# Down projections of a hybrid encoder layer: pair 17 in seven products in both runs, pair 19 in the second

## The chip, the core and the metric

The kernel runs on one core of a Trainium2 chip. Its engines work beside each other and meet at semaphores: TensorE (PE; its weight loads are shown as PEld), VectorE (DVE), ScalarE (ACT), GpSimd (POOL) and SyncE (SP). SP issues most of the transfers (DMA) from and to the chip's memory (DRAM). POOL issues those that add to what lies in on-chip memory already. The metric is the device time of one execution in microseconds (us).

## What is computed

One encoder layer for 256 tokens of width 2048 in float32. Two feed-forward layers (FFN 1 and FFN 2, hidden width 5632) stand around a mixer of a gated recurrence and windowed attention:

```python
def swiglu(x, w_gate_up, w_down):
    gate, up = jnp.split(x @ w_gate_up, 2, axis=-1)
    return (jax.nn.silu(gate) * up) @ w_down
...
ff = swiglu(rms_norm(x, pre_norm_ffn1[layer]), w_ffn1_gate_up[layer], w_ffn1_down[layer])
x = x + 0.5 * rms_norm(ff, post_norm_ffn1[layer])
...
mixed = jnp.concatenate([y_h.astype(x.dtype), y_a.astype(x.dtype)], axis=-1) @ w_mix_out[layer]
x = x + rms_norm(mixed, post_norm_mix[layer])
ff = swiglu(rms_norm(x, pre_norm_ffn2[layer]), w_ffn2_gate_up[layer], w_ffn2_down[layer])
x = x + 0.5 * rms_norm(ff, post_norm_ffn2[layer])
```

The change touches the down projections, `(silu(gate) * up) @ w_down`, of both FFNs: 256 x 5632 times 5632 x 2048.

## The kernel before

**Numbers in two parts.** Every float32 operand is split into a high part (a cast on ACT, tile `h`) and what is left (a subtraction on DVE, tile `l`); `split_act` (L176) does both, `split_half` (L169) for 1024 columns. A product of two operands is three matmuls, high by high, high by low and low by high (`three`, L452). All of them show line L458.

**Runs, pairs and steps.** A down projection goes over its output in two runs, columns 0 to 1023 and 1024 to 2047. The hidden width is cut into 22 pairs of 128-row blocks (`NU`), numbered 0 to 21. The lists `orders` (L1276) say in which order each run takes the pairs. A step is one pair in one run, so there are 44 steps; step i is at place i in the first run, and at place i - 22 in the second. One step's weights are one 1 MB load into a `raw` tile, and there are five such tiles. The hidden activations of a pair are a tile `ht`, already split. Pairs 0 to 7 are put away to DRAM and fetched again (`fetch_at`, L1382) into four tiles that take turns; the others stay in on-chip memory.

**Plain or in seven.** A plain pair multiplies its 2 x 2 blocks of tokens and rows with its blocks of columns one by one: 8 products, 24 matmuls (`play`, `plain`). A pair in seven uses a Strassen-like scheme with 7 products, 21 matmuls (`products` of `Blocks`, L505): sums of weight blocks and sums of token blocks are multiplied, some of the products go to four extra banks `p`, and `fold` (L533) adds these to the results once, after the last pair in seven. `as_seven` (L1290) says which pairs are done so: before the change the even ones 0 to 18 (`MIXED`) in both runs and 17 in the second.

**What a pair in seven needs.** The token sums (four sums of 128 x 128): for pairs 0 to 14 they are made while the hidden activations are, and kept in the place of the residual `X`; for 16, 17 and 18 `sums_again` (L1102) makes them on DVE, after the step that `again_at` (L1384) names. At each use they are split once more (`left_sums`, L657, tile `sp`). The weight sums: for pairs in `added` (L1281) `prepare` (L1310) first splits the first weight block (tiles `ha` and `la`, L1306; three of each) four steps ahead, and then POOL issues a transfer (L1314) that reads 0.5 MB of the weights once more and adds it to the upper half of `raw`. For the others DVE does that addition (L1337). In `splits` (L1320) the lower half of `raw` is then split (`l` of the lower half), the token sums too, two more additions follow on DVE (L1342, L1343), and then the upper half and the lower half again are split. So a pair in seven has three `h` and three `l` tiles of 1024 columns, a plain pair two of each; there are five tiles of either kind in all.

**Order of loads.** A `raw` tile is loaded anew as soon as its step's last split is through (`load_down`, L1293, on SP). Which step's weights come next is set by a list sorted by place, in which the pairs of `added` count as 3.5 places earlier:

```python
in_order = sorted(
    (i - 3.5 if u in added[r] else i, i) for i, (r, u) in enumerate(steps)
)
```

**Order of work.** The loop over the steps is written out by hand (`manual_schedule`): each engine does its instructions in the order in which the program states them. At step i it states: the first part of the splits of step i + 1, `prepare(i + 4)`, the fetches due at i, the rest of those splits for a plain pair, the products of step i, the rest of the splits for a pair in seven, and then the token sums due at i. After step 21 the first run's results are squared and scaled out of their banks (`second_run`, L721). Steps 42 and 43 (pairs 20 and 21) are held for the end, where the residual is added and the next stage begins (`finish`, L743). There the residual is loaded again (`new_x`) into the place where the token sums of pairs 0 to 14 lay.

Of the kernel before, what the change touches and what calls it, by code (L numbers as in the profile page):

```python
# [37 lines left out]
def hymba_layer_kernel(  # L38
# [900 lines left out]
    MIXED = range(0, 20, 2)  # L939
# [142 lines left out]
    def ffn(gated, w_dn, post_gain, again, gain=None, lead=None, aside=None):  # L1082

        with ExitStack() as st:
# [6 lines left out]
            hts, sums, away = [], {}, {}  # L1091
# [98 lines left out]
            def some(steps, n):  # L1190
                for _ in range(n):
                    next(steps)
# [21 lines left out]
            def boundary(g, ahead):  # L1214

                a, b = room_for("z"), room_for("s")
                c, (p1, p5, p6, p7) = gated.c, gated.p
                add = nc.vector.tensor_tensor
                rest_of = gated.take(g, last)

                def bank(m, n):
                    for k in range(2):
                        rest_of[4 * k + 2 * m + n]()

                nc.scalar.copy(a, p1)
                add(c[0][0], c[0][0], a, ALU.add)
                add(b, p6, a, ALU.add)
                add(a, p7, b, ALU.add)
                add(c[1][0], c[1][0], a, ALU.add)  # L1229
                bank(0, 0)  # L1230
                bank(1, 0)
                add(b, p5, b, ALU.subtract)
                add(c[0][1], c[0][1], b, ALU.add)
                bank(0, 1)
                add(b, p5, a, ALU.subtract)
                add(c[1][1], c[1][1], b, ALU.add)  # L1236
                bank(1, 1)
                some(ahead, 2)

            def first_pairs(g, waiting):  # L1240

                gated.group(g)
                some(waiting, 1)
                gated.prepare(g, MIXED_IN[1])
                some(waiting, 1)
                ahead = gated.splits(g, 1)
                some(ahead, 2)
                gated.prepare(g, MIXED_IN[2])
                for one in gated.take(g, 0):
                    one()  # L1250
                some(waiting, 1)
                ahead = gated.splits(g, 2)
                some(ahead, 2)
                some(waiting, 1)
                some(ahead, 1)
                for one in gated.take(g, 1):
                    one()

            def pair_ahead(g, u):

                ahead = gated.splits(g, u + 1)
                next(ahead)
                if u + 1 == MIXED_IN[1]:
                    gated.prepare(g, MIXED_IN[3])
                next(ahead)
                for one in gated.take(g, u):
                    one()
                for _ in ahead:
                    pass
                if g == 1 and u == 5:  # L1270
                    sums_in(MIXED_IN[3])
                if u == 5 and 1 < g <= AWAY // 2 + 1:
                    put_away(2 * g - 4)
                    put_away(2 * g - 3)

            orders = [  # L1276
                [9, 11, 8, 13, 10, 15, 12, 1, 0, 3, 14, 5, 16, 17, 2, 7, 4, 19, 6, 18, 20, 21],

                [2, 7, 4, 9, 6, 8, 11, 10, 13, 12, 17, 15, 0, 5, 14, 3, 16, 1, 18, 19, 20, 21],
            ]  # L1280
            added = {0: (12, 0, 14, 16, 2, 4, 6, 18), 1: (*MIXED, 17)}  # L1281
            steps = [(r, u) for r in range(2) for u in orders[r]]
            in_order = sorted(
                (i - 3.5 if u in added[r] else i, i) for i, (r, u) in enumerate(steps)
# [3 lines left out]
            rows = None  # L1288

            def as_seven(r, u):  # L1290
                return u in MIXED or r == 1 and u in added[1]

            def load_down(raw):  # L1293
                if coming and (coming[0] < NU + 19 or any(raw is one for one in gated.lasting)):
# [25 lines left out]
            def splits(i):  # L1320
                if i >= 2 * NU - Pairs.HELD:
                    return
                r, u = steps[i]
                raw = raws[i]
                parts = got[i] = []
                b11, b12, b21, b22 = blocks(raw)
                if not as_seven(r, u):
                    parts.append(split_half(raw, 0))
                    yield
                    parts.append(split_half(raw, 1))  # L1330
                    load_down(raw)
                    yield
                    return
                four = raw.rearrange("p (i c) -> p i c", i=4)
                if i not in firsts:
                    first_block(i)
                    nc.vector.tensor_tensor(  # L1337
                        four[:, 0:2], four[:, 0::3], four[:, 1:2].to_broadcast([P, 2, 512]), ALU.add
                    )
                parts.append(split_half(raw, 1))  # L1340
                rows.left_sums_ahead(u)
                nc.vector.tensor_tensor(b22, b11, b22, ALU.add)  # L1342
                nc.vector.tensor_tensor(b21, b22, b21, ALU.add)  # L1343
                yield
                parts.append(split_half(raw, 0))
                yield
                parts.append(split_half(raw, 1))
                load_down(raw)
                yield
# [13 lines left out]
            with tc.manual_schedule():  # L1363
                gated.prepare(1, MIXED_IN[0])
                some(gated.splits(1, 0), 2)
                for g in range(1, NG):
                    first_pairs(g, waiting)
                    for u in range(2, last - 1):
                        pair_ahead(g, u)
                    some(gated.splits(g, last), 2)  # L1370
                    if g < NG - 1:
                        gated.prepare(g + 1, MIXED_IN[0])
                    for one in gated.take(g, last - 1):
                        one()
                    boundary(g, gated.splits(g + 1, 0) if g < NG - 1 else splits(0))
                    waiting = units(gated.c, rest)
                    some(waiting, 2)
                room_cm.__exit__(None, None, None)
                close_far()
                back_cm = tc.tile_pool(name=nm("hb"), bufs=AWAY // 2, reuse_waits="tile")  # L1380
                back = back_cm.__enter__()
                fetch_at = {2: (1,), 3: (0,), 5: (3,), 6: (5,), 9: (2,), 10: (7,), 11: (4,), 13: (6,)}  # L1382
                fetch_at.update({25: (0,), 26: (5,), 28: (3,), 29: (1,)})
                again_at = {8: 16, 14: 18, 24: 17}  # L1384
                for u in MIXED[8:]:
                    sums[u] = None
                rows = Pairs(w_dn, orders, hts, sums, work, post_gain, near=MIXED[:2])
                rows.firsts = 3
                some(waiting, 2)
                ahead = splits(1)  # L1390
                some(ahead, 2)
                products(0)
                for _ in range(2):
                    load_down(back.tile([P, 2048], F32, tag="raw", name=nm("raw"), bufs=2))
                some(waiting, 1)
                ahead = splits(2)
                some(ahead, 2)
                some(waiting, 1)
                some(ahead, 1)
                products(1)  # L1400
                for i in range(2, 2 * NU - Pairs.HELD):
                    if i == NU + 18:
                        back_cm.__exit__(None, None, None)
                        early_cm.__exit__(None, None, None)
                        post = rows.post = st.enter_context(post_pool())
                    ahead = splits(i + 1)
                    next(ahead, None)
                    prepare(i + 4)
                    for u in fetch_at.get(i, ()):
                        fetch(u)  # L1410
                    next(ahead, None)
                    if i == NU + 18:
                        rows.hold(1, raws[2 * NU - 2])
                    products(i)
                    for _ in ahead:
                        pass
                    if i in again_at:
                        sums[again_at[i]] = sums_again(again_at[i])
                    if i == 8:
                        rows.half_gain(far["pool"])  # L1420
                    if i == NU - 1:
                        sums[17] = None
                        rows.second_run()
                        rows.fold_after(NU - Pairs.HELD - 1)
                fold = rows.fold()
                some(fold, 2)
                rows.hold(1, raws[2 * NU - 1])
                for _ in fold:
                    pass
# [951 lines left out]
```

## Time and profile before

| what | us |
|---|---|
| median of three runs | 1815.16 (1814.6 to 1816.67) |
| the profiled execution | 1816.97 |
| its span, first to last instruction | 1815.2 |
| FFN 1, first run, steps 0 to 21 | 476.5 to 590.1 |
| FFN 1, second run, steps 22 to 41 | 590.1 to 691.8 |
| FFN 2, first run, steps 0 to 21 | 1580.8 to 1694.5 |
| FFN 2, second run, steps 22 to 41 | 1694.5 to 1796.2 |

All times of the trace count from the first instruction of the profiled execution. In rows of time the columns are start, duration, engine, line, operation, output <- inputs, shapes, and in brackets how long the engine was idle before and what ended that. In rows of a stage the columns are the stage, its length, the busy time of PE, PEld, DVE, ACT and POOL with the number of instructions, the granted TensorE clock, the busy share of the 16 DMA engines, and GB/s; that share goes a little over 1 where transfers are dense. Matmul durations are those of a pipeline: each is shown with 389 ns, and the next begins 227 ns after it. The start of an `l` row and the next row's start show how long DVE was really taken.

### The profile page before, as it was taken

To read this page: it belongs to the slowest core of one execution; us is meant where nothing else is said; L and a number is where in the kernel's file an instruction comes from. 1 tells how busy PE (TensorE), PEld (TensorE's weight loads), DVE (VectorE), ACT (ScalarE), POOL (GpSimd) and SP (SyncE) were. 2 spreads that over 40 slices of the span, in tenths; PEclk is the share of its full clock that TensorE was granted. 3 is DMA by queue.
4 is the path that set the end of the run, shared out by engine and by line. 5 is a ranking of instruction groups with operands and counts; after the bars stand their busy time and mean duration, and the time that the engine had idled before them with its cause. 6 is when DMAs were issued, how large, how long until landed. Compare 5 with 4: busy or idle time off the path is not lost.

```text
span 1815.2 us, 23684 instructions
## 1 busy us (share of the span) xinstructions
PE 1802.6 (99%) x8412; PEld 1496.8 (82%) x8412; DVE 1645.7 (91%) x2149; ACT 1128.2 (62%) x1496; POOL 177.9 (10%) x168
## 2 busy tenths in 40 slices
PE   9999999999999999999999999999999999999998
PEld 7888888888888888888888888888888888888886
DVE  7999999999989988988888888899999999998987
ACT  7565666666565757556676666566666666566663
POOL 1011111111011100110000100111111111011110
PEclk9999999999999999999999999999999999999999
DMA  8889999999699996965655767889999998699994
GB/s 302 240 237 282 276 283 255 254 257 260 212 343 279 280 323 208 296 174 163 174 162 166 245 206 276 244 244 270 284 268 272 255 249 251 192 337 311 263 315 164
DMA packets 217335, 457.06 MB, mean 252 GB/s; under 512 B 13064, under 2 KB 49760, under 8 KB 215936
## 3 DMA queue, kind: packets, MB, share of 16 engines
q1 hardware_dynamic: 181600, 389.07, 61.6%
q0 software_dynamic: 35440, 66.21, 21.4%
q8 instruction: 66, 1.08, 0.2%
q14 instruction: 53, 0.43, 0.1%
q10 hardware_dynamic: 176, 0.27, 0.0%
HBM read 440.80 MB, written 14.70 MB: 251 GB/s over the span
## 4 chain that ended last, share of the span: by engine, by line
PE 88%; DMA 4%; DVE 4%; ACT 2%; issue 1%; SPq 0%; POOL 0%; DVEq 0%; ACTq 0%; POOLq 0%
PE pa L458 40%; PE pb L458 35%; PE pa L326 5%; PE pa L331 3%; DMA raw<-in_w_ffn_gate_up_dram 2%; DVE l L178 2%; DMA raw<-in_w_mix_in_dram 2%; ACT h L177 1%; PE pb L1728 1%; PE pa L1172 1%; PE pb L1172 1%; DMA vr<-in_w_mix_in_dram 1%; PE pa L381 0%; ACT xt L228 0%; PE pa L380 0%
## 5 line engine op out<-in xcount | busy, mean ns | idle before, releaser
L177 ACT CAST h<-raw 128x1024 fp32r<-128x1024 f32 (+1 forms) x846 | 833.0, 1011 | 455.7 <-PE pb L458 152.4
L178 DVE TENSOR_TENSOR l<-raw,h 128x1024 fp32r<-128x1024 f32 (+1 forms) x846 | 963.0, 1170 | 97.6 <-ACT h L177 79.1
L458 PE MATMUL pa<-h,xt 128*128 128x512 f32 x1194 | 418.9, 392 | 0.1
L458 PE MATMUL pb<-h,xt 128*128 128x512 f32 x1038 | 371.0, 392 | 0.4 <-DVE pb L1229 0.4
L458 PEld LDWEIGHTS pa<-h,xt 128*128 128x128 f32 x1194 | 224.2, 188 | 47.9 <-DVE xt L233 0.6
L458 PE MATMUL pa<-l,xt 128*128 128x512 f32 x597 | 233.1, 390 | 0.4 <-DVE l L178 0.4
L458 PEld LDWEIGHTS pb<-h,xt 128*128 128x128 f32 x1038 | 194.8, 188 | 46.5 <-DVE pb L1236 3.7
L458 PE MATMUL pb<-l,xt 128*128 128x512 f32 x519 | 202.3, 390 | 0.0
L1011 POOL DMA_DIRECT2D raw<-in_w_ffn_gate_up_dram x78 | 94.5, 1212 | 733.0 <-DVE l L178 656.9
L458 PE MATMUL pb<-h,ht 128*128 128x512 f32 x452 | 159.2, 389 | 0.0
L458 PE MATMUL pa<-h,ht 128*128 128x512 f32 x452 | 159.2, 389 | 0.0
L458 PEld LDWEIGHTS pa<-l,xt 128*128 128x128 f32 x597 | 112.2, 188 | 23.4 <-DVE l L178 1.7
L458 PE MATMUL pa<-h,xs 128*128 128x512 f32 x332 | 118.6, 389 | 0.0
L458 PE MATMUL pb<-h,xs 128*128 128x512 f32 x332 | 115.7, 389 | 0.0
L458 PEld LDWEIGHTS pb<-l,xt 128*128 128x128 f32 x519 | 97.5, 188 | 18.7
L326 PE MATMUL pa<-xt,h 128*128 128x512 f32 x448 | 109.9, 393 | 0.0
L458 PEld LDWEIGHTS pa<-h,ht 128*128 128x128 f32 x452 | 84.9, 188 | 17.7
L458 PEld LDWEIGHTS pb<-h,ht 128*128 128x128 f32 x452 | 84.8, 188 | 17.7
L326 PEld LDWEIGHTS pa<-xt,h 128*128 128x128 f32 x448 | 81.5, 188 | 15.3
L458 PE MATMUL pa<-l,ht 128*128 128x512 f32 x226 | 87.9, 389 | 0.0
L458 PE MATMUL pb<-l,ht 128*128 128x512 f32 x226 | 87.9, 389 | 0.0
L1314 POOL DMA_DIRECT2D raw<-in_w_ffn_down_dram x38 | 46.1, 1212 | 371.7 <-DVE la L178 320.7
(341 smaller groups left out, 2537.8 us busy)
## 6 DMA issues: line engine op xcount, KB each, us to landing
raw<-in_w_ffn_gate_up_dram SPq DMA_DIRECT2D x350, 512.0 KB, 5.9
raw<-in_w_ffn_down_dram SPq DMA_DIRECT2D x88, 1024.0 KB, 8.1
raw<-in_w_ffn_gate_up_dram POOLq DMA_DIRECT2D x78, 512.0 KB, 8.0
raw<-in_w_mix_in_dram SPq DMA_DIRECT2D x36, 1024.0 KB, 5.1
raw<-in_w_ffn_down_dram POOLq DMA_DIRECT2D x38, 512.0 KB, 10.3
ht<-away SPq DMA_DIRECT2D x24, 512.0 KB, 10.4
raw<-in_w_mix_out_dram SPq DMA_DIRECT2D x12, 1024.0 KB, 6.5
raw<-in_w_mix_in_dram SPq DMA_DIRECT2D x34, 256.0 KB, 5.3
```

Of the source, the lines that this page charges most:

```text
L177: nc.scalar.copy(hi, src)
L178: nc.vector.tensor_tensor(lo, src, hi.bitcast(F32), ALU.subtract)
L326: nc.tensor.matmul(slot[f], weights(hs, kk, f), xcol(xt, k), start=(k == 0), stop=(k == KT - 1))
L331: nc.tensor.matmul(slot[f][:, 0:T], weights(ls, kk, f), xcol(xt, kh * 8 + kk, 0), start=False, stop=False,)
L458: nc.tensor.matmul(self.bank(at), lhs, rhs, start=(n == 1), stop=n in (ends, self.of[at]), skip_group_check=n > ends,)
L1011: nc.gpsimd.dma_start(raw[:, 0:1024].rearrange("p (k c) -> p k c", k=2), self.source(u, g)[:, :, 1], accum_op=ALU.add,)
L1172: nc.tensor.transpose(bank[:, o : o + P], zs[m][:, k * P : (k + 1) * P], ident)
L1314: nc.gpsimd.dma_start(raws[i][:, 0:1024].rearrange("p (k c) -> p k c", k=2), Pairs.part(w_dn, u, r)[:, :, 512:1024], accum_op=ALU.add,)
L1728: nc.tensor.matmul(dst, left[a], right[b], start=first and i == 0, stop=last and i == 2)
```

## The change

Pair 17 is done in seven in the first run too, at place 7, right behind pair 12; it was plain, at place 13. In the second run pair 19 is done in seven, at place 16, right behind pair 16; it was plain, at place 19. The other pairs of the two lists are shifted to match. In the first run 2 and 7 change places as well, and in the second run the pairs from place 13 on are 14, 5, 16, 19, 3, 18, 1 where they were 5, 14, 3, 16, 1, 18, 19. Both new pairs are among the `added` ones, so their weight sums come by a transfer that POOL issues, and their loads move up in SP's list. The token sums of 17 are made after step 4 and no more after step 24, those of 19 after step 30. This holds for both FFNs, since they share the function.

```diff
             orders = [
-                [9, 11, 8, 13, 10, 15, 12, 1, 0, 3, 14, 5, 16, 17, 2, 7, 4, 19, 6, 18, 20, 21],
-
-                [2, 7, 4, 9, 6, 8, 11, 10, 13, 12, 17, 15, 0, 5, 14, 3, 16, 1, 18, 19, 20, 21],
+                [9, 11, 8, 13, 10, 15, 12, 17, 1, 0, 3, 14, 5, 16, 7, 2, 4, 19, 6, 18, 20, 21],
+
+                [2, 7, 4, 9, 6, 8, 11, 10, 13, 12, 17, 15, 0, 14, 5, 16, 19, 3, 18, 1, 20, 21],
             ]
-            added = {0: (12, 0, 14, 16, 2, 4, 6, 18), 1: (*MIXED, 17)}
+            added = {0: (12, 17, 0, 14, 16, 2, 4, 6, 18), 1: (*MIXED, 17, 19)}
...
             def as_seven(r, u):
-                return u in MIXED or r == 1 and u in added[1]
+                return u in MIXED or u == 17 or r == 1 and u in added[1]
...
-                again_at = {8: 16, 14: 18, 24: 17}
-                for u in MIXED[8:]:
+                again_at = {4: 17, 8: 16, 14: 18, 30: 19}
+                for u in (*MIXED[8:], 17):
                     sums[u] = None
...
                     if i == NU - 1:
-                        sums[17] = None
+                        sums[19] = None
                         rows.second_run()
```

## The prediction

> **What bounds the kernel now.** I read the page's busy times and queues first, then the busy time per stage of the two down projections (all their steps from the first product to the last), then the chain of waits and the engines' own waits there.
>
> ```profile
> PE 1802.6 (99%) x8412; PEld 1496.8 (82%) x8412; DVE 1645.7 (91%) x2149; ACT 1128.2 (62%) x1496; POOL 177.9 (10%) x168
> q1 hardware_dynamic: 181600, 389.07, 61.6%
> q0 software_dynamic: 35440, 66.21, 21.4%
> ```
> ```profile
> 476.48:590.10 113.62, 113.62 (x507) 94.21 (x506) 105.22 (x124) 68.72 (x81) 12.14 (x10) 1.00 0.96 310
> 590.10:691.80 101.70, 101.70 (x450) 83.99 (x449) 92.38 (x105) 66.39 (x81) 10.93 (x9) 1.00 0.91 290
> 1580.79:1694.50 113.71, 113.71 (x507) 94.30 (x506) 105.11 (x124) 68.71 (x82) 12.11 (x10) 1.00 0.96 310
> 1694.50:1796.20 101.70, 101.70 (x449) 83.98 (x449) 92.47 (x106) 64.40 (x79) 10.89 (x9) 1.00 0.85 269
> ```
> ```profile
> 1745.22 2.72 PE pa L458 x12
> ```
> ```profile
> PEld pa L458 <- DVE y L713: 0.3, 1, 0.3
> ```
> The four stage rows are first and second run of the first feed-forward layer (FFN 1), then of FFN 2: length, then busy time of PE, PEld, DVE, ACT and POOL, granted clock 1.00, DMA share, GB/s. PE is busy in all of it. Twelve products follow each other in 2.72 us in the chain, 0.227 us each, and the only wait that PE's side shows in a down projection is 0.3 us. So these stages last as long as their products are many. DVE works 93% and 91% of them, and the DMA share is 0.85 to 0.96: both are close behind.
>
> A busy column alone does not prove that. The Trainium skill's Trainium Kernel Development and Optimization, section Best Practices, says to judge the distance to the roofline by LDWEIGHTS rather than by matmul busy time; by its PEld share, 94.21 of 113.62, PE would have 17% of room and the change would be worth nothing (1815.2 us). I go by the count, twelve in 2.72 us without a wait, under which each product removed is time removed.
>
> **The change, part by part.** Steps are numbered 0 to 43 over both runs.
>
> *Products.* A plain pair takes 24, a pair in seven 21. Pair 17 in the first run and 19 in the second, in both layers: 4 x 3 = 12 products less, 12 x 0.227 = 2.72 us. The accumulated banks, the fold and its place (after step 20 and step 41) stay.
>
> *DVE work of a seven.* These rows in a row of time hold one whole step of an added pair (step 6) behind the last half of a plain one:
>
> ```profile
> 500.42 0.69 DVE L178 TENSOR_TENSOR la<-raw,ha 128x512 fp32r<-128x512 f32 x1
> 501.02 2.35 DVE L178 TENSOR_TENSOR l<-raw,h 128x1024 fp32r<-128x1024 f32 x2
> 503.30 0.69 DVE L178 TENSOR_TENSOR sp<-sums,sp 128x512 fp32r<-128x512 f32 x1
> 503.90 0.69 DVE L1342 TENSOR_TENSOR raw<-raw 128x512 f32<-128x512 f32 x1
> 504.62 0.69 DVE L1343 TENSOR_TENSOR raw<-raw 128x512 f32<-128x512 f32 x1
> 505.23 2.51 DVE L178 TENSOR_TENSOR l<-raw,h 128x1024 fp32r<-128x1024 f32 x2
> ```
> By the starts: la 0.60, each l 1.14, sp 0.60, L1342 0.72, L1343 0.61. A seven costs 0.60 + 3 x 1.14 + 0.60 + 0.72 + 0.61 = 5.95 us of DVE against 21 x 0.227 = 4.76 on PE; a plain pair 2.28 against 5.44. So each conversion adds 3.7 us to DVE. The stage rows leave 113.62 - 105.22 = 8.4 and 101.70 - 92.38 = 9.3: it fits. ACT gets three more casts and has over 35 us; POOL one more issue of some 1.2 us (12.14 us for 10).
>
> *Token sums.* One set:
>
> ```profile
> 521.34 0.68 DVE L1107 TENSOR_TENSOR su<-ht 128x512 f32<-128x512 f32 x1
> 523.03 0.29 DVE L1114 TENSOR_TENSOR su<-su 128x128 f32<-128x128 f32 x1
> 523.24 1.22 DVE L178 TENSOR_TENSOR l<-raw,h 128x1024 fp32r<-128x1024 f32 x1
> ```
> 1.90 us. Those of 17 leave step 24 for step 4, those of 19 are new at step 30. Leaving step 24 relieves the stretch where DVE has least; step 30 is followed by the one where it has most:
>
> ```profile
> 615.00:625.00 10.00, 10.00 (x46) 8.29 (x45) 9.90 (x12) 7.41 (x10) 1.30 (x2) 1.00 1.01 350
> 635.00:645.00 10.00, 10.00 (x46) 8.29 (x45) 7.36 (x9) 5.05 (x7) 0.00 (x0) 1.00 1.05 359
> ```
>
> *First run, the tight place: step 7.* Pairs 12 and 17 now stand side by side at 6 and 7, with the sums of 17 before them.
>
> ```profile
> 507.76 0.37 SPq L1298 DMA_DIRECT2D raw<-in_w_ffn_down_dram  x1
> 508.02 1.05 ACT L177 CAST h<-raw 128x1024 fp32r<-128x1024 f32 x1 [1.55 <-DMA raw<-in_w_ffn_down_dram]
> 513.41 0.39 PE L458 MATMUL pa<-h,ht 128*128 128x512 f32 x1
> ```
> DVE ends step 6 at 505.23 + 2.51 = 507.74. Ahead of that the change puts the sums (1.90), la of step 7, la of step 9 instead of step 8 (0.60 net), and up to 0.4 since pair 10's load now leaves one place later: 510.6. Step 7 then needs lower l, sp, L1342, L1343 and upper l, 4.21 us: 514.8. PE starts step 7 at 513.41 and reaches the upper half's low part after ten products, 515.68. Cover 0.9 us; the last half, by the same count, 1.05. From step 8, plain (2.28 against 5.44), DVE wins it back. If the cover is gone by x, PE stops for x, in each layer.
>
> *Second run, the tight place: pair 15, step 33.* In FFN 2 its load needs 13.7 us, and ACT, then DVE, then nearly PE wait:
>
> ```profile
> L1298 SPq DMA_DIRECT2D raw<-in_w_ffn_down_dram x1: 367/367/367, 1733.4 to 1733.4; - x1
> DMA to landing us min/median/max: 13.7/13.7/13.7
> ```
> ```profile
> 1747.20 1.05 ACT L177 CAST h<-raw 128x1024 fp32r<-128x1024 f32 x1 [3.19 <-DMA raw<-in_w_ffn_down_dram]
> 1748.28 1.23 DVE L178 TENSOR_TENSOR l<-raw,h 128x1024 fp32r<-128x1024 f32 x1 [3.02 <-ACT h L177]
> 1750.05 0.39 PE L458 MATMUL pa<-l,ht 128*128 128x512 f32 x1
> ```
> The low part is ready at 1749.51, used at 1750.05: 0.54 us. The order up to here is the old one. The new sums and the earlier la of pair 14, 2.50 us together, fit into DVE's idle 3.02; the load itself follows step 30, which comes up to 1.9 us sooner without the sums of 17. I take a cover of 0.5 to 1.5 us. Behind it pairs 0 and 14 stand side by side at 34 and 35, and 16 and 19 at 37 and 38. The plain step 33 wins DVE 5.44 - 2.28 = 3.2 us, two sevens take 2 x (5.95 - 4.76) = 2.4: from 0.5 there are 1.3 left after step 35, and plain step 36 wins 3.2 again before the next two.
>
> *Transfers.* Four more accumulating ones. Queue q0 took 21.4% of 1815.2 us for 66.21 MB, so 0.52 MB costs 3.08 us of the 16 engines, about a whole 1.05 MB load on q1 (61.6% for 389.07 MB: 3.01). Room is seen where the share falls:
>
> ```profile
> 515.00:525.00 10.00, 10.00 (x46) 8.28 (x45) 9.18 (x14) 6.26 (x8) 1.22 (x1) 1.00 1.06 326
> 565.00:575.00 10.00, 10.00 (x46) 8.29 (x45) 9.83 (x12) 6.44 (x8) 1.21 (x1) 1.00 0.77 255
> 585.00:595.00 10.00, 10.00 (x45) 8.01 (x45) 9.81 (x13) 6.62 (x14) 0.00 (x0) 1.00 0.68 203
> 595.00:605.00 10.00, 10.00 (x46) 8.29 (x45) 9.96 (x12) 7.82 (x11) 2.44 (x2) 1.00 0.82 193
> ```
> Against 1.06, three windows alone leave 2.9 + 3.8 + 2.4 = 9.1 us. Cost on PE: 0, if the queue is early enough at steps 7 and 33; at most 3.08 less the cover where it is not.
>
> *Queues and waits.*
>
> ```profile
> ht<-away SPq DMA_DIRECT2D x24, 512.0 KB, 10.4
> X<-in_x_dram SPq DMA_DIRECT2D x2, 1024.0 KB, 12.3
> ```
> On SP every plain load keeps its distance (let go by the split of the third step before its own). The fetches of pairs 2, 7, 4 and 6 wait for a reader one step later; the shortest way left is that of 7, from step 10 to 14, at least 4 x 4.76 = 19 us against 10.4. What stands behind a fetch on SP is the next load, which waits for a split that ends at about the same time; cost 0, at most the part of a step (up to 1 us) by which a reader is late, and that lies within the covers above. The reload of the residual is let go one step sooner, since pair 14 reads the last sums kept in its place at step 35: its two transfers join the loads of steps 36 to 39 earlier, and nobody reads them before the end of the run. A new wait of ACT: three first blocks may live at once, and at steps 15, 31 and 34 a fourth is asked for. ACT's cast then waits for the running step's first three products, 0.68 us into it; behind it stand DVE's la and the next upper half, done some 3.4 us later (two casts, la, l), at 4.1; PE needs that at 4.76 + 2.27 = 7.0. Hidden by 2.9 us.
>
> *Sum.* The profiled execution took 1816.97 us (span 1815.2): 1816.97 - 2.72 = 1814.25. The median of the runs shown, 1815.16, lies 1.81 below it, so **1812.4 us**.
>
> **The rivals.**
> 1. *The transfers have no room* (slower). Mechanism: each added accumulation pushes a load behind it back by its whole 3.08 us, at steps 7 to 10 and at 33 to 36. For it: 1.06 at 515 to 525, and ACT waiting 1.55 and 3.19 us for loads at the two tight places. Against: 9.1 us of room in the first run and before the second's rush. It decides once lateness exceeds the cover. Price: 2 x (3.08 - 0.9) + 2 x (3.08 - 0.5) = 9.5, less 2.72: 1821.9. The Trainium skill's DMA: Bandwidth & Descriptors, section Issuing engines are not separate DMA queues, speaks for it: transfers started by GpSimd and by SP run on the same 16 engines and interleave. The trace agrees in so far as loads take 13.7 us beside accumulations.
> 2. *DVE comes late at step 7.* The walk above has 0.9 us of cover and is made of eight durations; were the sums and la worth twice their extra, 2.5 us more, PE would stop 1.6 us in each layer: 1812.4 + 3.2 = 1815.6, no change.
> 3. *More than the products.* The sums taken out of step 24 and the earlier residual shorten something else. PE's only wait here is 0.3 us a layer, so the down projections give 1812.4 - 0.6 = 1811.8; to pass 0.2% one more us must come from the stage behind FFN 1: 1810.8.
>
> **How the numbers follow.** Forecast 0.67 (1811.6 to 1813.6), rival 1 0.16, rival 2 0.10, rival 3 0.07. A measurement of this kernel tells about 0.2%, 3.6 us, from no change. The forecast's 2.72 is below that and rival 2 too: same 0.77. Rival 3: faster 0.07. Rival 1: slower 0.16. The range starts 0.6 under rival 3's first figure, at 1811.2, and runs up through rival 2 to a price of rival 1 cut to some 60% (1812.4 + 5.6), 1818.0: about 0.16 is left out, most of it rival 1 in full.
>
> **What would show it.** The product count falls by 12 to 8400, and the four stages shorten by 0.68 us each with PE busy throughout. Rival 1: PE idle at steps 7 to 10 or 33 to 36, released by an l that waited for a load, and longer times to landing there. Rival 2: the same idle time at step 7 with DVE busy before it. The forecast is wrong if PE shows more than 2 us of new waits in the down projections.

## The result and the profile after

The changed kernel takes 1827.75 us (median of six runs, 1827.46 to 1829.97) against 1815.66 for the kernel before in six runs beside it: a ratio of 1.0067, with a 95% interval of 1.0057 to 1.0078. That is slower by some 12 us, where 1812.4 was forecast. The profiled execution took 1827.75 us, its span 1826.0. The page of the changed kernel, busy times and the queue of the accumulating transfers:

```profile
PE 1804.9 (99%) x8400; PEld 1497.0 (82%) x8400; DVE 1661.3 (91%) x2179; ACT 1134.2 (62%) x1508; POOL 182.8 (10%) x172
q0 software_dynamic: 36528, 68.30, 21.9%
```

The twelve products are gone (8412 became 8400), and the four accumulating transfers are there (66.21 MB became 68.30). PE is nevertheless busy 2.3 us longer than before, and the span has 10.8 us more. The busy time by stage, whole down projections before (first to last product with hidden activations, held steps included), columns as in the prediction:

```profile
476.48:702.88 226.40, 226.40 (x1005) 187.39 (x1004) 207.58 (x243) 140.26 (x171) 23.63 (x20) 1.00 0.93 297
1580.79:1806.71 225.92, 225.92 (x1001) 186.97 (x1000) 204.12 (x240) 135.17 (x165) 23.56 (x20) 1.00 0.87 279
```

After, each down projection is cut: FFN 1's first run, second run up to a pause, and what is behind it; FFN 2's first run, and its second run up to the end of step 41:

```profile
475.24:590.00 114.76, 113.60 (x505) 93.51 (x503) 109.25 (x134) 69.10 (x84) 13.36 (x11) 1.00 0.98 311
590.00:691.21 101.21, 100.98 (x445) 83.07 (x443) 89.78 (x103) 65.16 (x80) 12.13 (x10) 1.00 0.90 286
691.21:711.83 20.62, 14.19 (x53) 11.39 (x53) 16.49 (x23) 8.96 (x16) 0.56 (x1) 0.75 0.51 175
1588.79:1706.03 117.24, 115.25 (x504) 94.71 (x504) 110.09 (x134) 69.62 (x85) 13.30 (x11) 0.99 0.96 305
1706.03:1806.87 100.84, 100.84 (x445) 83.25 (x444) 95.55 (x110) 66.87 (x81) 12.12 (x10) 1.00 0.88 276
```

FFN 1's down projection lasts 236.6 us in place of 226.4, FFN 2's (to 1817.47) 228.7 in place of 225.9: together 12.9 us more. The stages around them are 2.1 us shorter, which tells nothing: the start of FFN 1's alone lies anywhere from 474.8 to 476.7 in the profiles of this study. The two runs do not lose alike. Both first runs are longer than the 113.62 and 113.71 of before, though they have three products fewer. The second run of FFN 2 alone, 100.84 with PE busy throughout, is what was forecast (101.70 less 0.68). And the third row holds a pause and a granted clock of 0.75. PE's longest own waits in the changed kernel, FFN 1's down projection and then FFN 2's (total, times, longest):

```profile
PE pa L458 <- DVE pa L555: 6.4, 1, 6.4
PE pa L458 <- DVE l L178: 1.0, 1, 1.0
```
```profile
PE pa L458 <- DVE l L178: 2.0, 1, 2.0
```

From start to start of products, less the 0.227 us of one, the pauses are 6.59 us at the end of FFN 1's second run and 1.20 and 2.15 us at step 16 of the first runs. Products at a lower clock behind two of them make most of what is left.

**The pause of 6.59 us.** The timelines of SP and ACT, then DVE, then PE in the changed kernel, at the end of FFN 1's second run:

```profile
683.59 0.37 SPq L153 DMA_DIRECT2D raw<-in_w_mix_in_dram  x1
```
```profile
681.26 1.05 ACT L177 CAST h<-raw 128x1024 fp32r<-128x1024 f32 x1 [1.68 <-PE pb L458]
688.68 3.89 ACT L177 CAST h<-raw 128x1024 fp32r<-128x1024 f32 x4 [6.37 <-PE pa L458]
692.48 0.57 ACT L548 COPY y<-pa 128x512 f32<-128x512 f32 x1
692.96 1.99 ACT L177 CAST h<-raw 128x1024 fp32r<-128x1024 f32 x2
```
```profile
689.76 4.63 DVE L178 TENSOR_TENSOR l<-raw,h 128x1024 fp32r<-128x1024 f32 x4 [6.19 <-ACT h L177]
694.31 0.68 DVE L549 TENSOR_TENSOR y<-pb,y 128x512 f32<-128x512 f32 x1
...
696.96 0.69 DVE L555 TENSOR_TENSOR pa<-pa,y 128x512 f32<-128x512 f32 x1
```
```profile
690.98 0.39 PE L458 MATMUL pb<-h,ht 128*128 128x512 f32 x1
697.80 0.77 PE L458 MATMUL pa<-h,ht 128*128 128x512 f32 x1 [6.43 <-DVE pa L555]
698.36 0.63 PE L458 MATMUL pa<-l,ht 128*128 128x512 f32 x1
```

Before, ACT did the same part so:

```profile
681.83 2.95 ACT L177 CAST h<-raw 128x1024 fp32r<-128x1024 f32 x3 [1.68 <-PE pb L458]
684.69 0.57 ACT L548 COPY y<-pa 128x512 f32<-128x512 f32 x1
685.16 2.00 ACT L177 CAST h<-raw 128x1024 fp32r<-128x1024 f32 x2
```

Before, the cast at 681.83 is the last one of step 41, and the two behind it are the held step 42; then come the copy that begins the fold and the held step 43. After, the last cast of step 41 is followed by 6.37 us of nothing and then by four casts: two are the first split of the next stage's weights (`mix_in`), stated behind step 41's in the program as it was built, and the held steps stand behind them. Those weights were asked for at 683.59 and took 5.0 us to land, which gives 688.6; the cast begins at 688.68. (The row puts the wait down to a product of PE, but PE ends one every 0.227 us there. In the first experiment below, where the same two casts come behind the held steps, their wait is put down to this load.) ACT takes its work in order, so the held splits, the copy and with them the fold on DVE (L549 to L555) come 7.8 us later, and the held products need the banks that the fold writes. FFN 2 of the same execution has the same order of pairs and tiles and no next stage whose weights are split there:

```profile
1796.92 2.95 ACT L177 CAST h<-raw 128x1024 fp32r<-128x1024 f32 x3 [1.68 <-PE pb L458]
1799.78 0.58 ACT L548 COPY y<-pa 128x512 f32<-128x512 f32 x1
```

There the old order stands, 7 us ahead of step 41's end, and PE does not pause.

**The pauses at step 16.** The load of step 18 (pair 6), the accumulating transfers next to it, then ACT and DVE in FFN 1's first run after the change:

```profile
L1298 SPq DMA_DIRECT2D raw<-in_w_ffn_down_dram x1: 378/378/378, 535.6 to 535.6; - x1
...
DMA to landing us min/median/max: 14.7/14.7/14.7
```
```profile
L1314 POOL DMA_DIRECT2D raw<-in_w_ffn_down_dram x2: 1203/1215/1227, 534.9 to 540.1; - x2
```
```profile
550.40 0.62 ACT L177 CAST ha<-raw 128x512 fp32r<-128x512 f32 x1 [3.83 <-DMA raw<-in_w_ffn_down_dram]
```
```profile
551.05 0.69 DVE L178 TENSOR_TENSOR la<-raw,ha 128x512 fp32r<-128x512 f32 x1 [1.58 <-ACT ha L177]
...
559.86 5.76 DVE L178 TENSOR_TENSOR l<-raw,h 128x1024 fp32r<-128x1024 f32 x5
```

Before, the three loads issued between 530 and 548 took (shortest, median, longest):

```profile
DMA to landing us min/median/max: 9.3/9.5/10.7
```

The first of the three, issued at 531.7, was that of step 18 and took 10.7 us. Now it leaves at 535.6 and takes 14.7, so it lands at 550.3 in place of 542.4. It leaves later, and one reason is in SP's list: the load of step 15 now stands ahead of it (pair 2, counted 3.5 places earlier; before, the plain pair 7 stood at step 15). Two accumulations, of the neighbours at steps 15 and 16 (pairs 2 and 4), start 0.7 us ahead of it and 4.5 us behind. ACT waits 3.83 us for it, to split a block of step 18 while PE is in step 14. DVE idles behind ACT; from 551.05 it works almost without a break (one of 0.26 us) and still has step 16's upper half ready too late.

### The profile page after: what moved, and what is told of

Same layout as the page of the kernel before. It is cut to its first block, busy times and chain, and to the rows that moved or that the text cites. A ratio compares the mean times of both kernels' runs of the same rounds, so it can differ in the third digit from the quotient of the medians.

```text
span 1826.0 us, 23727 instructions
## 1 busy us (share of the span) xinstructions
PE 1804.9 (99%) x8400; PEld 1497.0 (82%) x8400; DVE 1661.3 (91%) x2179; ACT 1134.2 (62%) x1508; POOL 182.8 (10%) x172
## 3 DMA queue, kind: packets, MB, share of 16 engines
q0 software_dynamic: 36528, 68.30, 21.9%
## 4 chain that ended last, share of the span: by engine, by line
PE 84%; DVE 10%; issue 2%; DMA 2%; ACT 1%; DVEq 0%; ACTq 0%; POOL 0%; POOLq 0%
PE pa L458 38%; PE pb L458 33%; PE pa L326 5%; DVE l L178 5%; PE pa L331 3%; DMA raw<-in_w_ffn_down_dram 1%; ACT h L177 1%; PE pa L381 1%; PE pa L380 1%; PE pa L379 1%; DVE la L178 1%; PE pb L1728 1%; DVE raw L1342 1%; DVE sp L178 1%; PE pa L1172 0%
## 5 line engine op out<-in xcount | busy, mean ns | idle before, releaser
L458 PE MATMUL pa<-h,ht 128*128 128x512 f32 x428 | 153.4, 395 | 6.6 <-DVE pa L555 6.4
L458 PE MATMUL pb<-h,ht 128*128 128x512 f32 x428 | 151.4, 390 | 0.0
L458 PEld LDWEIGHTS pb<-h,ht 128*128 128x128 f32 x428 | 80.6, 188 | 16.8
L1314 POOL DMA_DIRECT2D raw<-in_w_ffn_down_dram x42 | 50.9, 1212 | 373.3 <-DVE la L178 373.3
L458 PE MATMUL pb<-l,ht 128*128 128x512 f32 x214 | 83.4, 390 | 0.0
```

The costliest lines, as they stand in the source:

```text
L458: nc.tensor.matmul(self.bank(at), lhs, rhs, start=(n == 1), stop=n in (ends, self.of[at]), skip_group_check=n > ends,)
L1314: nc.gpsimd.dma_start(raws[i][:, 0:1024].rearrange("p (k c) -> p k c", k=2), Pairs.part(w_dn, u, r)[:, :, 512:1024], accum_op=ALU.add,)
```

## The experiments

The theory is that of the last section: the order of ACT's work at the end of FFN 1, and a late load ahead of step 16. Each expectation names its own theories with their letters. The times are medians beside runs of the kernel before in the same session (1815.86, 1816.28 and 1816.34 in the three sessions). "Gaps" are added up over a down projection: each start of a product that comes more than 0.24 us after the one before counts with what is over 0.227 us; before has 0.31 us in FFN 1 and 0.23 in FFN 2, the changed kernel 11.8 and 4.2.

**1. Another pair last.** Pairs 1 and 15 exchanged in the second run.

```diff
-  [2, 7, 4, 9, 6, 8, 11, 10, 13, 12, 17, 15, 0, 14, 5, 16, 19, 3, 18, 1, 20, 21],
+  [2, 7, 4, 9, 6, 8, 11, 10, 13, 12, 17, 1, 0, 14, 5, 16, 19, 3, 18, 15, 20, 21],
```


> The changed kernel with pairs 1 and 15 exchanged in the second run: 1 at step 33, 15 at step 41; loads keep their places in the list. Theory A: the stall of 6.6 us at the end of FFN 1 comes from pair 1 being last. Its activations lie in one of the four fetched tiles, and the held pairs' splits (steps 42 and 43) go into room that is given free only when these tiles are; so on ACT and DVE they stand behind the split of the next stage's weights, whose load lands at 688.58. Then the stall and the low granted clock behind it (0.62 and 0.53 from 692 to 704) go, and the time falls by 9 to 10 us to about 1817.5 to 1818.5; the stalls at 559.7 (FFN 1, 1.2 us) and 1673.6 (FFN 2, 2.2 us) stay. Rival B: the held splits are late since the load of step 43 now follows the split of step 40 and no longer that of 39. Nothing in that is touched here, so the stall stays and the time is 1827 to 1828.

Measured 1819.0 us, ratio 1.0017 (1.0007 to 1.0026), 0.5 us above the expected range. ACT has its old order again, and the two casts of `mix_in` come behind the held steps:

```profile
682.03 2.95 ACT L177 CAST h<-raw 128x1024 fp32r<-128x1024 f32 x3 [1.67 <-PE pb L458]
684.89 0.57 ACT L548 COPY y<-pa 128x512 f32<-128x512 f32 x1
...
691.68 2.00 ACT L177 CAST h<-raw 128x1024 fp32r<-128x1024 f32 x2 [4.22 <-DMA raw<-in_w_mix_in_dram]
```

The pause of 6.59 us and the low clock behind it are gone, so it hung on the pair that stands last; pauses of 1.98 and 2.15 us at step 16 stay, and about 0.3 and 0.4 us where the runs change. Experiments 4 to 6 start from this kernel, with gaps of 3.13 and 3.55 us.

**2. The two runs apart.** The second run's part of the change alone, and the first run's alone.

```diff
 (second run only)
-  added = {0: (12, 17, 0, 14, 16, 2, 4, 6, 18), 1: (*MIXED, 17, 19)}
+  added = {0: (12, 0, 14, 16, 2, 4, 6, 18), 1: (*MIXED, 17, 19)}
-  again_at = {4: 17, 8: 16, 14: 18, 30: 19}
+  again_at = {8: 16, 14: 18, 24: 17, 30: 19}
 (first run only)
-  added = {0: (12, 17, 0, 14, 16, 2, 4, 6, 18), 1: (*MIXED, 17, 19)}
+  added = {0: (12, 17, 0, 14, 16, 2, 4, 6, 18), 1: (*MIXED, 17)}
-  again_at = {4: 17, 8: 16, 14: 18, 30: 19}
+  again_at = {4: 17, 8: 16, 14: 18}
```

The other run has the order and the choice of pairs of before in each.

> Only the second run's part of the change (pair 19 in seven, the new order with pair 1 last); the first run is as before, with pair 17 plain at step 13, and the sums of 17 are made after step 24 again. Theory A: the 6.6 us at the end of FFN 1 stay, those at 559.7 and 1673.6 go with what follows them (1.2, 2.2 and 1.8 us of lower clock), six products come back (1.4 us): 1827.75 - 5.2 + 1.4 = about 1824. Theory that the transfers have no room anywhere: stalls of over 1 us also at steps 33 to 36.

> Only the first run's part (pair 17 in seven at step 7, its sums after step 4, 7 before 2); the second run is as before, without 17's sums after step 24. No stall at the end of FFN 1; stalls stay at steps 16 of FFN 1 (1.2 us) and FFN 2 (2.2 us and 1.8 us of lower clock); six products less: 1815.66 - 1.4 + 5.2 = about 1819.5. If the first run's stalls came from the second run's part, for example by its loads, the time would be 1814.3.

The second run alone: 1823.74 us, 1.0041 (1.0026 to 1.0055), with a pause of 6.90 us at the end of FFN 1 and none over 0.3 in FFN 2. The first run alone: 1820.76 us, 1.0027 (1.0017 to 1.0037), with pauses of 1.91 and 2.18 us at step 16 and none at the end. The two losses are independent and each belongs to its run; the second figure is 1.3 us above what was expected.

**3. The next stage's split behind the held ones.** The changed kernel, pair 1 last, with one edit elsewhere:

```diff
     def load(self):
-        self.parts = [split(raws[0]), ([], [])]
+        self.parts, self.soon = None, raws[0]
...
     def more(self, i):
+        if self.parts is None:
+            self.parts = [split(self.soon), ([], [])]
```


> The changed kernel with one edit: the first split of the next stage's weights is stated inside the ordered block, behind the splits of the held steps 42 and 43. Pair 1 stays last. Theory A (only the order of ACT's work makes the stall of 6.59 us at the end of FFN 1's second run; FFN 2, which has no such split, has none with the same order of pairs): the stall is gone, the granted clock stays at 1.00 behind it, FFN 1 lasts 228 to 229 us; 1818.5 to 1820. Rival B (the fetched tile of pair 1 is in use until the end of step 41, and the held splits need its room): the held splits still start at some 3 us before the end of step 41 or later, 4 us or more of the stall stay; 1822 to 1826.

Measured 1820.55 us, 1.0021 (1.0012 to 1.0030). ACT and the clock at the same place:

```profile
683.22 2.96 ACT L177 CAST h<-raw 128x1024 fp32r<-128x1024 f32 x3 [1.68 <-PE pb L460]
686.09 0.57 ACT L550 COPY y<-pa 128x512 f32<-128x512 f32 x1
```
```profile
692.00:698.00 6.00, 6.00 (x28) 4.95 (x28) 4.07 (x7) 1.91 (x4) 0.00 (x0) 1.00 0.94 326
```

The pause is gone with pair 1 last, so the room of pair 1 does not hold the held splits up on the chip (rival B falls): the place of the two casts in ACT's queue, with DVE's subtractions behind them, made it. FFN 1 lasts 229.61 us and the time is 1820.55, each some 0.6 over what was expected: the pause of 2.18 us at step 16 was followed by products at a lower clock this time, and behind the held steps, at 703.9, there is a pause of 0.5 us that the others do not have. The pause at step 16 differs between profiles even where the first run is the same: 1.20 us in FFN 1 and 2.15 in FFN 2 in the changed kernel, 1.98 and 2.15 in the first experiment, 1.91 and 2.18 in the second, 2.18 and 1.12 here. Differences of under 1 us between two profiles therefore say little.

**4. DVE or transfers?** Two kernels move work of ACT and DVE away from the tight place: the sums of 18 after step 17 in place of 14; and the first blocks of steps 18 and 19 one step later.

```diff
 (sums of 18 later)
-  again_at = {4: 17, 8: 16, 14: 18, 30: 19}
+  again_at = {4: 17, 8: 16, 17: 18, 30: 19}
 (first blocks later)
-  prepare(i + 4)
+  if i not in (14, 15):
+      prepare(i + 4)
+  if i in (15, 16):
+      prepare(i + 3)
```


> As e1, and the token sums of pair 18 are made after step 17 instead of after step 14. Theory C: PE stops in step 16 because DVE comes late: ACT's first-block cast of step 18 waits 3.8 us for its load, and DVE, set back by that, makes the sums of 18 (1.9 us) just ahead of step 16's splits. Moving the sums takes 1.9 us out of the row, so the stall of 1.2 us in FFN 1 goes and that of 2.2 us in FFN 2 is at most 0.3: 4 to 5 us less than e1, 1812.5 to 1814. Rival D: PE waits for the load of step 16 or its accumulation themselves, and the sums only fill a wait: the time of e1 within 1 us.

> As pair 1 early, and the first blocks of steps 18 and 19 are split one step later than the others. Theory A (ACT and DVE take their work in the order stated, and the first block of step 18, whose load comes late, holds up what is stated behind it, the splits of step 16 among it): the stall at step 16, 1.98 and 2.15 us with pair 1 early, falls under 0.5 in each layer, and about 1815.5 to 1816.5 follows, unless step 18 is late in its turn. Theory B (DVE has too much work at steps 14 to 19, whatever the order): the gaps of the first run keep their sum of 2.7 to 3.1 us in each layer and only move behind step 16; 1818 to 1819.

Sums later: 1818.76 us, 1.0016 (1.0007 to 1.0025). The pause at step 16 falls to 0.42 and 0.79 us, but 0.5 us appears at step 19 and 1.55 where the runs change: gaps of 3.46 and 3.87 us beside 3.13 and 3.55. First blocks later: 1820.9 us, 1.0029 (1.0019 to 1.0038): none at step 16, but 1.6 and 1.4 at step 19 and 1.55 at the change of runs, gaps of 4.0 and 3.7; DVE now waits 3.3 us for an accumulation that leaves later. Moving the work moves the pause, and neither edit gained anything on the first experiment. The times that theory C (1814 at most) and theory A (1816.5 at most) expected were both missed; rival D had the time of the first edit, but not that the pause would move. I read this so: what DVE is behind by step 14 it stays behind.

**5. Other neighbours.** Pairs 7 and 2 exchanged in the first run, so that 2 and 4 are no longer side by side.

```diff
-  [9, 11, 8, 13, 10, 15, 12, 17, 1, 0, 3, 14, 5, 16, 7, 2, 4, 19, 6, 18, 20, 21],
+  [9, 11, 8, 13, 10, 15, 12, 17, 1, 0, 3, 14, 5, 16, 2, 7, 4, 19, 6, 18, 20, 21],
```


> As pair 1 early, and pairs 7 and 2 of the first run exchanged: ... 5, 16, 2, 7, 4, 19 ..., so that pairs 16 and 2 are neighbours in place of 2 and 4. Theory A (late load of pair 6 at step 18, accumulations of steps 15 and 16 close together): accumulations of steps 14 and 16 are a step further apart, the load of step 18 lands 2 to 3 us sooner and the stall at step 16 falls under 1 us; 1816 to 1817.5. Theory B (too much DVE work, any order): the first run's gaps stay at 2.7 to 3.1 us in each layer and appear a step sooner; 1818.5 to 1819.5.

Measured 1818.8 us, 1.0015 (1.0006 to 1.0024): the load of step 18 still takes 15.6 us, the pause splits in two (1.03 and 0.82 us), the gaps are 3.20 and 3.39. That pairs 2 and 4 are neighbours is not the cause; the time is the one of theory B.

**6. Fewer bytes.** Pair 4 of the first run added up by DVE (L1337) in place of a transfer; the same with the fetch of pair 6 two steps later; and every accumulation of the first run cut to half.

```diff
 (pair 4 by DVE)
-  added = {0: (12, 17, 0, 14, 16, 2, 4, 6, 18), 1: (*MIXED, 17, 19)}
+  added = {0: (12, 17, 0, 14, 16, 2, 6, 18), 1: (*MIXED, 17, 19)}
 (and the fetch)
-  11: (4,), 13: (6,)}
+  11: (4,), 15: (6,)}
 (half accumulations)
+  n = 2 if r else 1
-      raws[i][:, 0:1024].rearrange("p (k c) -> p k c", k=2),
-      Pairs.part(w_dn, u, r)[:, :, 512:1024],
+      raws[i][:, 0 : n * 512].rearrange("p (k c) -> p k c", k=n),
+      Pairs.part(w_dn, u, r)[:, 0:n, 512:1024],
```


> As pair 1 early, and pair 4 of the first run (step 16) is added up by DVE: no first block split ahead, no accumulating transfer, its load 3.5 places later in the list. Theory A (the transfers are full between steps 12 and 18, one accumulation is 3.08 us of them): the load of step 18 takes about 11 to 12 us in place of 14.7, the first block of step 18 is through before step 16 needs ACT, the stall at step 16 is under 0.5; 1815.5 to 1816.5. Theory B (DVE has too much work there): no fewer operations on DVE, so the first run's gaps keep 2.7 us or more in each layer; 1818 to 1820.

> As pair 1 early with pair 4 added up by DVE, and the fetch of pair 6 at step 15 in place of 13. Theory A (transfers between steps 12 and 18): 0.5 MB less ahead of the load of step 18, about 1.5 us, so the stall at step 16 falls from 0.8 to under 0.3 us in each layer, total gaps about 1.2; 1815.3 (1 us less than with pair 4 alone). Theory B (DVE's debt): the stall stays at 0.7 to 0.9; 1816 to 1816.8.

> As pair 1 early; in the first run each accumulating transfer adds only the first of its two row blocks (0.25 MB in place of 0.5 MB), so half of the weight sums of the first run's added pairs are left out. All work of ACT, DVE and PE stays. Theory A (transfers: the late load of step 18 leaves DVE idle for 3.3 + 0.9 us between 535 and 545, and that is what it lacks at step 16): 9 x 1.5 us of the 16 engines fall away, the load of step 18 lands 3 to 4 us sooner, no gap of PE over 0.4 us at step 16, gaps under 1 us in each layer; 1814 to 1815.5. Theory B (DVE's own work is too much in the first run): the stall at step 16 stays at 1.5 us or more; 1817.5 to 1819.

Pair 4 by DVE: 1816.38 us, 1.0000 (0.9991 to 1.0009). The load of step 18 takes 12.4 us, the pause 0.80 in both layers, the gaps are 1.94 and 1.89. The time is in the range of theory A, but its "under 0.5" for the pause missed; the addition on DVE that the edit puts there, 1.15 us at 554.91, is of the size of what is left. The later fetch on top: 1816.31 us, 1.0001 (0.9991 to 1.0010), with the pause unchanged at 0.8. That is what theory B expected, but the edit brought the load only from 12.4 to 11.9 us, so it says little.

Half accumulations, a kernel that leaves out half of the weight sums of the first run's added pairs and so does not compute the layer: 1812.95 us, 0.9981 (0.9971 to 0.9990), 1 us under the expected range. Both down projections, then the load of step 18:

```profile
476.70:701.75 225.05, 225.05 (x1000) 186.19 (x999) 215.40 (x258) 143.97 (x178) 22.96 (x22) 1.00 0.91 293
1579.40:1804.00 224.60, 224.60 (x995) 185.81 (x994) 211.71 (x255) 138.67 (x171) 22.88 (x22) 1.00 0.86 275
```
```profile
L1298 SPq DMA_DIRECT2D raw<-in_w_ffn_down_dram x1: 378/378/378, 537.5 to 537.5; - x1
...
DMA to landing us min/median/max: 10.6/10.6/10.6
```

DVE does as much as in the first experiment (258 and 255 instructions in both), and PE has no pause at all. The load is back at 10.6 us. What DVE waited for in FFN 1's first run, in the first experiment and then in this one:

```profile
DVE l L178 <- ACT h L177: 3.8, 3, 3.3
DVE la L178 <- ACT ha L177: 0.9, 1, 0.9
```
```profile
DVE l L178 <- ACT h L177: 1.7, 3, 0.8
DVE la L178 <- ACT ha L177: 0.3, 1, 0.3
```

The two long waits, 3.3 and 0.9 us, both lie between 535 and 552 and are gone. The 0.9 stands behind the load of step 18. The 3.3 stands behind another one, that of step 14 (pair 7), which left at 532.8 and took 11.6 us in the first experiment; ACT waited for it so:

```profile
544.44 1.05 ACT L177 CAST h<-raw 128x1024 fp32r<-128x1024 f32 x1 [3.67 <-DMA raw<-in_w_ffn_down_dram]
```

With half accumulations it took 8.1 us. So with the same work DVE is in time once the transfers are cut: the transfers were the cause, by late loads, and DVE's lateness followed from them. The theory of too much work on DVE, whose times experiment 5 and the later fetch had met, does not explain this. Whether less work on DVE would have absorbed the late loads too was not tried. And the stages are shorter than before by 226.40 - 225.05 = 1.35 and 225.92 - 224.60 = 1.32 us, which is the forecast's 6 x 0.227 = 1.36 in each layer.

**7. What fits.** The first run with the order and pairs of before; the second with 17 and 19 in seven and pair 1 early; sums of 17 after step 4, kept apart until the second run.

```diff
-  added = {0: (12, 17, 0, 14, 16, 2, 4, 6, 18), 1: (*MIXED, 17, 19)}
+  added = {0: (12, 0, 14, 16, 2, 4, 6, 18), 1: (*MIXED, 17, 19)}
-  sums[again_at[i]] = sums_again(again_at[i])
+  (kept if i == 4 else sums)[again_at[i]] = sums_again(again_at[i])
-  sums[19] = None
+  sums[17], sums[19] = kept[17], None
```


> First run with the orders of before (pair 17 plain), second run with pairs 17 and 19 in seven and pairs 1 and 15 exchanged; token sums of 17 after step 4, kept apart until the second run, those of 18 after step 14, of 19 after step 30. Six products fewer than before in all, 6 x 0.227 = 1.36 us. Theory A (the first run's debt comes with pair 17 in seven there, and the second run with pair 1 early holds): no gap over 0.3 us in either layer, 1815.8 - 1.4 = 1814.4. Theory B (pair 19 in the second run has no room either): gaps of 1 us or more at steps 35 to 41; 1816.5 or more.

Measured 1814.52 us (11 runs), 0.9990 (0.9981 to 0.9999) against 1816.28:

```profile
475.55:701.27 225.72, 225.72 (x1002) 186.82 (x1001) 212.38 (x253) 142.54 (x175) 24.84 (x21) 1.00 0.94 300
1579.09:1804.35 225.26, 225.26 (x998) 186.41 (x997) 209.16 (x250) 137.38 (x168) 24.76 (x21) 1.00 0.88 283
```

PE is busy throughout, and the stages are 0.68 and 0.66 us shorter than before: three products each. It computes all of the reference and is the best of those that do, though by less than the 0.2% that a measurement can tell safely.

## Why the prediction was wrong

**The sum was right, the covers were not.** "12 x 0.227 = 2.72 us" holds: with the transfers cut and pair 1 early, the two down projections give 1.35 + 1.32 = 2.67 us. (The time of that kernel, 1812.95, is 3.4 us under the kernel before beside it; the 0.7 beyond the 2.67 lie outside these stages or in the noise, so that it nearly meets the 1812.4 is in part luck.) The other reading, by PEld's 83% of a stage, under which the change was worth nothing, did not hold. DVE's terms (5.95 for a seven, 1.90 for a set of sums) were, if anything, too high: in the same kernel DVE's busy time is 7.8 and 7.6 us above that of before, where 2 x 3.7 + 1.9 = 9.3 was forecast for each layer. The work was costed rightly and hidden wrongly, in two places.

**First failed step: "The accumulated banks, the fold and its place (after step 20 and step 41) stay."** The place stays, but the pair at step 41 changed from 19 to 1. I read that as a change of names. In the program as built it put two casts ahead of the held splits in ACT's queue, and the forecast did not list what stands between step 41's splits and the fold. It cost 6.59 us of pause and some 3 us of products at a lower clock, in FFN 1 only: the largest part of the loss, and in none of the rivals. Experiments 1 and 3 show it, each by undoing one side. What stays argued is why the order came out so: pair 1 lies in one of the four tiles for fetched pairs, whose room the held splits are given after step 40, and the pairs that stand last in the kernel before and in experiment 1 (19 and 15) do not. A step of the manual order that has to wait for room would then let work from outside that order go first.

**Second failed step: "Cost on PE: 0, if the queue is early enough at steps 7 and 33".** Those two steps held: the changed kernel has no pause at either, the walk's cover of 0.9 us at step 7 was enough, and rival 2 fell. But the 9.1 us of room were added up from windows at 515 to 525 as the full reference and at 565 to 605 as the room, that is, behind the place where it was wanted. Between them, where the loads of steps 14 and 18 run after the change, the share was at its top before it already:

```profile
535.00:545.00 10.00, 10.00 (x46) 8.29 (x45) 8.28 (x9) 6.20 (x7) 1.20 (x1) 1.00 1.05 337
545.00:555.00 10.00, 10.00 (x46) 8.29 (x45) 9.02 (x14) 6.72 (x8) 1.23 (x1) 1.00 1.06 337
```

The added accumulation and the rearranged ones raised the load of step 18 from 10.7 us to 14.7, and it also left 3.9 us later, which the forecast did not count either. DVE lost some 4 us there that it could not win back before the end of the run: by the forecast's own terms it works 105.22 + 3.7 + 1.9 = 110.8 of 112.9 us (109.95 of 113.30 with half accumulations). Price: 1.98 and 2.15 us at step 16 with 0.7 and 0.8 at the change of runs (experiment 1, gaps of 6.7 us less 0.5 as before).

**Rival 1 had the mechanism and the wrong steps.** It said "steps 7 to 10 and 33 to 36" and 9.5 us of pauses. Transfers did run out of room, once in each layer, for 6.1 us; with the forecast's 1812.4 that makes 1818.5, and experiment 1 measured 1819.0. The rule that was cited beside it, from the Trainium skill's DMA: Bandwidth & Descriptors, section Issuing engines are not separate DMA queues (transfers of GpSimd and SP share the same 16 engines and interleave), agrees with the runs: halving GpSimd's transfers of the first run alone took SP's load of step 18 from 15.5 us in experiment 1 to 10.6.

**The new wait of ACT for a fourth first block** never set a pause. ACT's waits for a first block in the changed kernel's first run of FFN 1 (total, times, longest) are for loads alone:

```profile
ACT ha L177 <- DMA raw<-in_w_ffn_down_dram: 6.3, 3, 3.8
```

What I had not priced is the other wait of such a cast. It is stated four steps ahead, and when its load is late it holds up everything of nearer steps behind it.

**What would show it.** The count of 8400 came true; "the four stages shorten by 0.68 us each with PE busy throughout" came true in one of four, FFN 2's second run, and the limit of 2 us of new waits was passed.

## What to carry to other kernels

When a reordering changes which item stands last before a hand-over between stages, list what each engine does from its last own instruction to the first of the next stage, in the order of the program as built: one foreign instruction that waits for its own load can cost more than all that the change saves. Room on the transfer engines is counted at the step that needs it and ahead of it, never as a sum over the run; and a load that is put earlier in a list makes the ones behind it leave later. And work that is prepared several steps ahead in an in-order queue is only cover as long as its load is early; a late one makes it a barrier, and shifting the work behind it moves the pause without shortening it.

## What the runs showed of the hardware

PE paid for the pause a second time. Behind it, in windows of 6 us of the changed kernel:

```profile
692.00:698.00 6.00, 0.20 (x1) 0.23 (x2) 5.93 (x9) 2.94 (x4) 0.00 (x0) 0.62 0.76 272
698.00:704.00 6.00, 6.00 (x15) 4.69 (x16) 3.71 (x5) 0.71 (x3) 0.00 (x0) 0.53 0.68 232
704.00:710.00 6.00, 6.00 (x28) 4.94 (x27) 4.23 (x7) 4.17 (x7) 0.56 (x1) 1.00 0.05 20
```

At a granted clock of 0.53 PE starts 15 products in 6 us, 0.43 us apart (697.80, then 698.36 and 698.79 for the next two of its rows), against 28 at 1.00; it lasts until 703.5 us, 5.7 us after PE started again, and costs some 3 us. The Trainium skill's TensorE: Matmul & The Clock Gate, section Part 1: The HAM clock gate (the "warmup" mystery), says that PE falls to half its clock after an idle window of about 3.4 us and comes back after a busy one. The fall after the pause of 6.59 us agrees, and so does the 6.90 us one of the second run alone, with a clock of 0.50 in the 6 us that begin 0.6 us before PE starts again. The return took longer here than one such window.

Shorter pauses do not follow so simply. After 2.15 us at step 16 of FFN 2 the changed kernel shows this, and the first experiment after the same 2.15 us that:

```profile
1676.00:1680.00 4.00, 4.00 (x11) 3.14 (x12) 4.00 (x4) 3.62 (x5) 0.38 (x1) 0.57 0.72 121
```
```profile
1667.00:1670.00 3.00, 2.68 (x12) 2.19 (x13) 3.00 (x4) 3.00 (x5) 0.76 (x1) 1.00 0.46 68
```

Pauses of 2.15 and, in experiment 3, 2.18 us were followed by eight or nine products at half speed, some 1.7 us; pauses of 1.91, 1.98, 2.15 and 2.18 in other kernels were not. So a pause of some 2 us, well under 3.4, can cost nearly its own length again. What decides it was not tried.
